# Moving a join: Fourier matmuls ahead of the last z tiles, and a third bank for the decay exponents

## The chip, the cores and the metric

The kernel runs on one core of a Trainium2 chip. The metric is the device time of one execution in microseconds. A core has a matrix engine (TensorE, PE in the profile), three engines for elementwise work (VectorE or DVE, ScalarE or ACT, GpSimd or POOL) and a synchronising engine (SyncE or SP), from whose queue this kernel issues every DMA. Matmul results go to PSUM, which has eight banks of 512 float32 columns for each of the 128 partitions; all other tiles lie in SBUF.

## The reference

One layer of a diffusion backbone over 2048 latent tokens with a prefix of 256 context tokens. The input is normalised and projected to 5168 columns (u, zf, zs, x/B/C, dt). The Fourier group takes the real part of a two-dimensional DFT of u, a linear map, and a gate silu(zf). The other group runs a 3x3 depthwise convolution and a bidirectional chunked state-space scan with 24 heads in four groups, gated with silu(zs) and normalised in groups. Both are joined and projected once more, with a residual and a last norm.

```python
decay within a chunk:  y_diag = (C B^T * exp(segsum(a))) x
decay from the state:  y_off  = C h * exp(a_cum)
gated  = (y_f + y_b + d_skip * x) * silu(zs)
ssd    = gated * rsqrt(mean(gated^2) + eps) * norm_w      # mean over 384 channels of a group
four   = (real(fft2(u)) @ w_fourier + b_fourier) * silu(zf)
out    = rmsnorm(x + gate * ([four, ssd] @ w_out)) * final_norm_w
```

## The kernel before, in words

Matrix products that need float32 accuracy are made of three matmuls on values that are split into a high and a low part (`hi*hi + lo*hi + hi*lo`). So a weight tile is loaded raw (`raw`, one buffer of 512 KB), ACT copies its high part (`wh`) and POOL subtracts to the low part (`wl`); the normalised input lies in `hh` and `hl` in four blocks of 512 tokens each.

The stages are: context; projections of dt and of the scan's inputs; convolution; the backward scan, with z tiles (the projection to zs, 128 channels by 512 tokens each, 24 matmuls) of the blocks 0 to 2 interleaved; the Fourier part, with the 12 z tiles of block 3 interleaved; and the last stage. Before that last stage the split columns of the output projection, 32 loads of 512 KB, are read back from DRAM (`wo_d`) into the places of `hh` and `hl` that have become free (`wplace`, four groups of eight loads, `w_group(g)`).

The Fourier part has a first step (`f_table`, `f_step2`; the L923 transforms) and 16 calls `f_mm(dt, h, i)` of 12 matmuls (L941 to L943); after each second call `f_gate` (L951, L960) multiplies into `zf`, which was loaded by `zf_load` from `zfT_d`, and after the last of a `dt` the result, 1 MB, is stored to `fm_d`. `interleave(main, side, lead, speed, finish)` writes the operations of two lists in turn by a table of costs; what of the side list is not placed comes back as `left`.

The last stage goes over 16 chunks times 4 groups, 64 units u. Each has six steps. `s1`: loads; the decay exponents as two matmuls for each half (`parg`, L1079), joined by a predicated copy on DVE (L1081), exponential on ACT (L1083), product with C B^T on DVE (w, L1084). `s2`: loads; the part from the state (`pyo`, L1115 to L1117), scaled (L1119) and added to the backward part on POOL (L1120). `s3`: the state update (`pst`, L1136 to L1138). `s4`: y of the unit, 12 matmuls and three transposes that add the part of s2 (`py`, L1151 and L1154), then the gate on DVE (`gt`, L1157), squares on ACT, a reduction on DVE. `s5`: the norm. A matmul with ones sums over the partitions (`pn`, L1167), ACT takes a root by three activations (L1170 to L1172), DVE mends it by two instructions (L1173, L1174) that write into pn, and multiplies the gated tile by it (L1176); the product is split into `mh` and `ml`. `s6`: the unit's share of the output projection, 24 matmuls (`po`, L1210 to L1212), from mh, ml and the Fourier operand `fm`. The loop writes s1 and s2 of u+1, s3 and s4 of u, s5 of u-1 and s6 of u-2 in each turn.

The written order isn't the executed one: a scheduler orders the instructions of each engine by its own estimate of durations, under the dependencies of the tiles. A tile with `bufs=1` may be written again only when its last reader is done. `issue_after(x)` holds loads back behind x. Each engine keeps its order on the chip.

In the last stage the eight PSUM banks are: parg 2, po 2, pyo 2 (with pst), py 1, pn 1.

Of the kernel before, what the change touches and what calls it, by code (L numbers as in the profile page):

```python
# [18 lines left out]
P = 128  # L19
D = 1024  # L20
# [29 lines left out]
def mixer_layer(ctx: ExitStack, tc: tile.TileContext, A: dict, out: bass.AP, taps=None):  # L50
# [797 lines left out]

    wos = {}
    worder = [k for g in range(G) for k in (4 + 3 * g, 5 + 3 * g, 6 + 3 * g, g)]  # L850
    wplace = [((hl, 1536), (hh, 1536)), ((hl, 0), (hl, 1024)), ((hl, 512), (hh, 1024)), ((hh, 0), (hh, 512))]

    def w_load(n):
        r, k = 2 * (n % 4), worder[n]
# [4 lines left out]
    def w_group(g):  # L859
        for n in range(4 * g, 4 * g + 4):  # L860
            w_load(n)
# [148 lines left out]
    for b in range(4):  # L1010
# [5 lines left out]
    side.append((0.0, f_switch))  # L1016
    fmm = [(dt, h) for dt in dts[:2] for h in range(2)] + [(dt, h) for h in range(2) for dt in dts[2:]]
    for n, (dt, h) in enumerate(fmm):
        if n in (4, 5):
            side.append((0.0, zf_load(dt)))  # L1020
        if n == 6:
            side.append((0.0, lambda: w_group(1)))
# [23 lines left out]
    ps = pool("ps2", space=PSUM)  # L1046
    fo["new"] = lambda: ps.tile([P, 512], F32, name="pft", tag="out", bufs=2)
    pre2 = preload(LNEXP)
    units = {}

    def s1(u):
# [16 lines left out]
        cb = wa1.tile([P, P], F32, name="cb", tag="cb")  # L1068
        load(cb, cb_d[c, :, g])
        chl = wa1.tile([P, 2, P], F32R, name="chl", tag="chl")  # L1070
        load(chl[:].bitcast(F32), chl_d[c, :, g].bitcast(F32))
        d["chl"] = chl
        w = wa1.tile([P, HG, P], F32, name="w", tag="w")
        for h2 in range(2):
            cols = slice(384 * h2, 384 * h2 + 384)
            pa = []
            for dr in range(2):
                po = ps.tile([P, 3, P], F32, name="parg", tag="arg", bufs=2)
                mm(po, l[:, dr], r[:, cols], start=True, stop=True)  # L1079
                pa.append(po)  # L1080
            nc.vector.copy_predicated(out=pa[0], mask=msk[:].unsqueeze(1).broadcast_to([P, 3, P]), data=pa[1])  # L1081
# [7 lines left out]
    pfb.close()  # L1089
    p1w.close()  # L1090
    wk = pool("wk", 2)
    fnw = const_tile("fnw", wk)
    wa = pool("wa", 2)

    def s2(u):
        c, g = divmod(u, G)
        d = units[u]
        gs = slice(g * GW, (g + 1) * GW)
        yb = wa1.tile([P, HG, 64], F32, name="yb4", tag="yb")
        load(yb[:].rearrange("p h w -> p (h w)"), yb_d[c, :, gs])  # L1100
        zs = wa1.tile([P, 3, P], F32, name="zs4", tag="zs")
        load(zs, zsT_d[c, :, 3 * g:3 * g + 3, :])
        d["zs"] = zs
        xg = wa1.tile([P, HG, 64], F32, name="xg", tag="xg", bufs=3)
        load(xg[:].rearrange("p h w -> p (h w)"), xtok_d[c, :, gs])
        d["x"] = xg
        bt = wa1.tile([P, 2, P], F32R, name="bt4", tag="bt", bufs=2)
        d["ld"] = load(bt[:].bitcast(F32), bhl_d[c, :, g].bitcast(F32))
        d["b"] = bt
# [5 lines left out]
        mm(po, d["chl"][:, 0], sh, start=True, stop=False)  # L1115
        mm(po, d["chl"][:, 0], sl, start=False, stop=False)
        mm(po, d["chl"][:, 1], sh, start=False, stop=True)  # L1117
        ec = d["sml"][:, 2, g * HG:(g + 1) * HG].unsqueeze(2).broadcast_to([P, HG, 64])
        nc.vector.tensor_tensor(out=ts, in0=po, in1=ec, op=ALU.mult)  # L1119
        nc.gpsimd.tensor_tensor(out=ts, in0=ts, in1=yb, op=ALU.add)  # L1120
        d["ts"] = ts

    def s3(u):
# [21 lines left out]
    def s4(u):  # L1145
        c, g = divmod(u, G)
        d = units[u]
        py = ps.tile([P, 3, P], F32, name="py", tag="yT", bufs=1)
        for h in range(HG):
            o = 64 * (h % 2)  # L1150
            mm(py[o:o + 64, h // 2, :], d["x"][:, h], d["w"][:, h], start=(h < 2), stop=False, skip_group_check=True)  # L1151
        tsf = d["ts"][:].rearrange("p h w -> p (h w)")
        for j in range(3):
            mm(py[:, j, :], tsf[:, j * P:(j + 1) * P], ident, is_transpose=True, start=False, stop=(j == 2),  # L1154
               skip_group_check=True)
        gt = wk.tile([P, 3, P], F32, name="gt", tag="gt")
        nc.vector.scalar_tensor_tensor(out=gt, in0=py, scalar=-1.0, in1=d["zs"], op0=ALU.mult, op1=ALU.mult)  # L1157
        sq = wk.tile([P, 3, P], F32, name="sq4", tag="sq", bufs=1)
        nc.scalar.activation(sq, gt, AF.Square)
        s0 = wk.tile([P, P], F32, name="s0", tag="s0", bufs=1)  # L1160
        nc.vector.tensor_reduce(out=s0, in_=sq[:].rearrange("p j l -> p l j"), axis=AX.X, op=ALU.add)
        d["gt"], d["sq"] = gt, s0

    def s5(u):
        d = units[u]
        pn = ps.tile([P, P], F32, name="pn", tag="misc", bufs=1)
        mm(pn, ones, d["sq"], start=True, stop=True)  # L1167
        rs = wk.tile([P, P], F32, name="rs4", tag="rs", bufs=1)
        tt = wk.tile([P, P], F32, name="tt", tag="tt", bufs=1)
        nc.scalar.activation(rs, pn, AF.Ln, bias=eps_t[:, 0:1], scale=1.0 / GW)  # L1170
        nc.scalar.activation(rs, rs, AF.Exp, scale=-0.5)
        nc.scalar.activation(tt, rs, AF.Square, scale=math.sqrt(0.5 / GW))  # L1172
        nc.vector.scalar_tensor_tensor(out=pn, in0=pn, scalar=EPS * GW, in1=tt, op0=ALU.add, op1=ALU.mult)  # L1173
        nc.vector.scalar_tensor_tensor(out=pn, in0=pn, scalar=1.5, in1=rs, op0=ALU.subtract, op1=ALU.mult)  # L1174
        mx = d["gt"]
        nc.vector.tensor_tensor(out=mx, in0=mx, in1=pn[:].unsqueeze(1).broadcast_to([P, 3, P]), op=ALU.mult)  # L1176
# [14 lines left out]
    def s6(u):  # L1191
# [14 lines left out]
        for i, q in [(i, q) for i in range(2) for q in range(4)] if (u > NU-2) else [(i, q) for q in range(4) for i in range(2)]:  # L1206
                k, a, b = ops[q]
                wh, wl = wos[k]
                po = ost["po"][i]
# [38 lines left out]
    for u in range(NU + 2):  # L1248
        if u + 1 < NU:
            if u > 0:  # L1250
                s1(u + 1)
            s2(u + 1)
        if u < 2:
            with tc.issue_after(fo["st"]), tc.issue_after(units[u + 1]["ld"]):
                w_group(u + 2)
        if u < NU:
            s3(u)
            s4(u)
        if 1 <= u <= NU:
            s5(u - 1)  # L1260
        if u >= 2:
            s6(u - 2)
# [110 lines left out]
```

## Time and profile before

| | |
|---|---|
| runs | 1903.54, 1904.05, 1899.87 us; median 1903.54 |
| profiled execution | 1907.05 us, its span 1905.3 us, mean granted PE clock 0.978 |
| PE busy | 1810.8 us, 95% of the span |
| DVE, ACT, POOL busy | 1259.1, 874.9, 904.0 us |
| DMA | 301.8 MB, 158 GB/s in the mean |
| last stage | from 1260 us to the end |

In the rows of the profile a line such as `L1151` is one of the kernel before. `out<-in` names the tiles, `x12` counts instructions that were merged into a row, `[15.64 <-DVE yy L951]` is the engine's idle time ahead of the row and what ended it. A stretch's row gives its length, then for PE, PE's weight loads, DVE, ACT and POOL the busy time with the count of instructions, then the clock that PE was granted (1.00 is full speed), the share of the DMA engines and GB/s.

### The profile page before, as it was taken

To read this page: it belongs to the slowest core of one execution; us is meant where nothing else is said; L and a number is where in the kernel's file an instruction comes from. 1 tells how busy PE (TensorE), PEld (TensorE's weight loads), DVE (VectorE), ACT (ScalarE), POOL (GpSimd) and SP (SyncE) were. 2 spreads that over 40 slices of the span, in tenths; PEclk is the share of its full clock that TensorE was granted. 3 is DMA by queue.
4 is the path that set the end of the run, shared out by engine and by line. 5 is a ranking of instruction groups with operands and counts; after the bars stand their busy time and mean duration, and the time that the engine had idled before them with its cause. 6 is when DMAs were issued, how large, how long until landed. Compare 5 with 4: busy or idle time off the path is not lost.

```text
span 1905.3 us, 28132 instructions
## 1 busy us (share of the span) xinstructions
PE 1810.8 (95%) x9142; PEld 1495.8 (79%) x9142; DVE 1259.1 (66%) x1809; ACT 874.9 (46%) x1968; POOL 904.0 (47%) x791
## 2 busy tenths in 40 slices
PE   7989999999999999999999999957999999999997
PEld 3779988888888888788888877845778777777875
DVE  4744578888898887556666622334677777767865
ACT  4532244445445445347666643312444444434443
POOL 2320034223124133178788723235777777668742
PEclk9999999999999999999999999977999999999999
DMA  8332345445446245467777764786444444444441
GB/s 306 127 95 78 96 135 169 144 130 160 128 125 194 90 138 159 143 196 216 209 218 212 221 232 136 245 277 208 123 146 149 130 132 135 148 122 137 145 136 48
DMA packets 291332, 301.80 MB, mean 158 GB/s; under 512 B 34098, under 2 KB 242066, under 8 KB 290675
## 3 DMA queue, kind: packets, MB, share of 16 engines
q1 hardware_dynamic: 291186, 300.01, 50.6%
q8 instruction: 73, 1.20, 0.3%
q14 instruction: 73, 0.59, 0.1%
HBM read 196.82 MB, written 103.10 MB: 157 GB/s over the span
## 4 chain that ended last, share of the span: by engine, by line
PE 72%; DMA 9%; POOL 4%; DVE 3%; issue 2%; ACT 2%; SPq 1%; POOLq 0%; ACTq 0%; DVEq 0%
PE pj L178 11%; PE pj L177 11%; PE pj L176 11%; PE po L1212 6%; PE po L1210 6%; PE po L1211 6%; PE py L1151 2%; PE parg L1079 2%; POOL sl L72 2%; PE pj L508 1%; PE pj L509 1%; PE pj L510 1%; PE py L1154 1%; DMA ev<-in_wout 1%; PE ptr L569 1%
## 5 line engine op out<-in xcount | busy, mean ns | idle before, releaser
L178 PE MATMUL pj<-hh,wl 128*128 128x512 f32 x1152 | 453.9, 394 | 0.8 <-POOL wl L72 0.8
L176 PE MATMUL pj<-hh,wh 128*128 128x512 f32 x1152 | 450.7, 395 | 3.9 <-ACT img L68 2.1
L177 PE MATMUL pj<-hl,wh 128*128 128x512 f32 x1152 | 453.3, 393 | 0.0
L636 DVE SCALAR_TENSOR_TENSOR pacc<-img,c_convw,pacc 128x1024 f32<-128x1024 f32 x320 | 410.4, 1288 | 60.2 <-ACT pacc L633 50.7
L72 POOL TENSOR_TENSOR wl<-raw,wh 128x1024 fp32r<-128x1024 f32 x48 | 115.6, 2409 | 348.7 <-ACT wh L68 296.2
L178 PEld LDWEIGHTS pj<-hh,wl 128*128 128x128 f32 x1152 | 217.2, 189 | 48.3 <-issue 1.6
L176 PEld LDWEIGHTS pj<-hh,wh 128*128 128x128 f32 x1152 | 217.4, 189 | 46.7 <-ACT img L68 3.2
L177 PEld LDWEIGHTS pj<-hl,wh 128*128 128x128 f32 x1152 | 217.4, 189 | 40.3 <-issue 1.0
L807 ACT ACTIVATE xd<-xt,smb 128x64 f32<-128x64 f32 x384 | 100.9, 336 | 80.1 <-POOL yb L811 78.7
L1210 PE MATMUL po<-hl,mh 128*128 128x512 f32 x288 | 118.7, 412 | 1.0 <-DVE og L1224 0.6
L1211 PE MATMUL po<-hh,mh 128*128 128x512 f32 x288 | 115.0, 399 | 0.0
L1081 DVE COPY_PREDICATED parg<-msk,parg 128x384 f32<-128x384 uint8 x128 | 71.2, 556 | 65.9 <-PE parg L1079 65.4
L1212 PE MATMUL po<-hl,ml 128*128 128x512 f32 x288 | 110.6, 403 | 2.5 <-POOL ml L72 2.4
L1083 ACT ACTIVATE w<-parg 128x384 f32<-128x384 f32 x128 | 62.2, 486 | 108.3 <-DVE parg L1081 108.0
L72 DVE TENSOR_TENSOR xl<-xw,xh 128x384 fp32r<-128x384 f32 x76 | 63.7, 842 | 59.4 <-ACT xh L68 58.0
L1120 POOL TENSOR_TENSOR ts<-ts,yb 128x384 f32<-128x384 f32 x64 | 73.3, 1145 | 57.9 <-issue 30.4
L1079 PE MATMUL parg<-rt,lt 128*128 128x384 f32 x256 | 87.7, 371 | 11.8 <-DMA lt<-q_d 7.5
L72 POOL TENSOR_TENSOR ml<-gt,mh 128x384 fp32r<-128x384 f32 x64 | 68.2, 1065 | 58.9 <-ACT mh L68 55.5
L68 ACT ACTIVATE xh<-xw 128x384 fp32r<-128x384 f32 x136 | 70.0, 516 | 50.2 <-PE pst L1138 17.0
L1084 DVE TENSOR_TENSOR w<-w,cb 128x768 f32<-128x768 f32 x64 | 81.0, 1265 | 12.0 <-ACT w L1083 10.8
L72 POOL TENSOR_TENSOR sl<-ev,sh 128x512 fp32r<-128x512 f32 x32 | 42.4, 1324 | 89.6 <-DMA wo_d<-sl 36.0
L72 DVE TENSOR_TENSOR sl<-hbk,sh 128x384 fp32r<-128x384 f32 x64 | 60.0, 939 | 37.4 <-ACT sh L68 37.3
(388 smaller groups left out, 4131.9 us busy)
## 6 DMA issues: line engine op xcount, KB each, us to landing
raw<-in_win SPq DMA_DIRECT2D x48, 512.0 KB
xt<-xtok_d SPq DMA_DIRECT2D x80, 192.0 KB
xtok_d<-tk SPq DMA_DIRECT2D x48, 256.0 KB
zsT_d<-ev SPq DMA_DIRECT2D x48, 256.0 KB
yb_d<-yb SPq DMA_DIRECT2D x64, 192.0 KB
yb<-yb_d SPq DMA_DIRECT2D x64, 192.0 KB
zs<-zsT_d SPq DMA_DIRECT2D x64, 192.0 KB
xg<-xtok_d SPq DMA_DIRECT2D x64, 192.0 KB
```

The source lines that it names most:

```text
L72: (lo_engine or nc.vector).tensor_tensor(out=lo, in0=src, in1=hi.bitcast(F32), op=ALU.subtract)
L176: mm(po, wh[:, k], a, start=(k == 0), stop=False)
L177: mm(po, wh[:, k], b, start=False, stop=False)
L178: done["mm"] = mm(po, wl[:, k], a, start=False, stop=(k == KT - 1)).ins
L636: nc.vector.scalar_tensor_tensor(out=acc, in0=im[:, r0 + dy:r0 + dy + 16, dx:dx + GRID_W], scalar=tap(t), in1=acc, op0=ALU.mult, op1=ALU.add)
L807: nc.scalar.activation(xd[:, h], d["x"][:, h], AF.Copy, scale=smb[:, 3, c, g * HG + h:g * HG + h + 1])
L1079: mm(po, l[:, dr], r[:, cols], start=True, stop=True)
L1084: nc.vector.tensor_tensor(out=w, in0=w, in1=cb[:].unsqueeze(1).broadcast_to([P, HG, P]), op=ALU.mult)
L1120: nc.gpsimd.tensor_tensor(out=ts, in0=ts, in1=yb, op=ALU.add)
L1210: mm(po, a, wh[:, i], start=(g == 0 and q == 0), stop=False)
L1211: mm(po, a, wl[:, i], start=False, stop=False)
L1212: mm(po, b, wh[:, i], start=False, stop=(g == 3 and q == 3))
```

## The change

Four parts. (1) The Fourier preparation is interleaved with the z tiles 0 to 4 of the 12, the 16 `f_mm` calls with the tiles 5 to 7, and the tiles 8 to 11 come last; under them go the loads of the output projection's groups 0 and 1. `wplace` is reordered, so that block 3's columns, which those last tiles still read, belong to group 3. Loads of the first units stand ahead of the last tiles, for which the loads are split out of `s1` and `s2` (`s1_load`, `s2_load`). Groups 2 and 3 are held back behind the units' loads, and no longer behind the Fourier store. `fnw` is loaded in the third turn. (2) parg gets a third bank (`arg0` two, `arg1` one). (3) pn has no bank of its own: `py` becomes four times 128 columns, and pn of unit u-1 is written in the fourth of py of unit u. (4) s6 takes the Fourier operand first, and the last unit's order follows.

```diff
-    wplace = [((hl, 1536), (hh, 1536)), ((hl, 0), (hl, 1024)), ((hl, 512), (hh, 1024)), ((hh, 0), (hh, 512))]
+    wplace = [((hl, 0), (hl, 1024)), ((hl, 512), (hh, 1024)), ((hh, 0), (hh, 512)), ((hl, 1536), (hh, 1536))]
...
-    left = interleave(zs_ops([(i, (3,)) for i in range(19, 7, -1)]), side, 10, .75)
+    ztiles = list(zs_ops([(i, (3,)) for i in range(19, 7, -1)]))
+    ztiles = [ztiles[n:n + KT + 1] for n in range(0, len(ztiles), KT + 1)]
+    zrun = lambda a, b: [op for t in ztiles[a:b] for op in t]
+    interleave(zrun(0, 5), side, 8, 1, True)
+    f_switch()
+    side = []
...
         side += [(2.6, f_mm(dt, h, i)) for i in range(2)]
+        if n in (1, 3):
+            side.append((0.0, zf_load(dts[2 + n // 2])))
+    interleave(zrun(5, 8), side, 0, 1, True)
...
-    w_group(0)
-    for _, fn in left:
-        fn()
-    p1.close()
...
+    s1_load(0)
+    s2_load(0)
+    s1_load(1)
+    interleave(zrun(8, 12), [(1.0, lambda n=n: w_load(n)) for n in range(8)], 0, 1, True)
+    p1.close()
+    ps = pool("ps2", space=PSUM)
+    pre2 = preload(LNEXP)
...
-                po = ps.tile([P, 3, P], F32, name="parg", tag="arg", bufs=2)
+                po = ps.tile([P, 3, P], F32, name="parg", tag=f"arg{dr}", bufs=2 - dr)
...
-    fnw = const_tile("fnw", wk)
+    fnw = wk.tile([P, D], F32, name="c_fnw", bufs=1)
...
-        py = ps.tile([P, 3, P], F32, name="py", tag="yT", bufs=1)
+        py = d["py"] = ps.tile([P, 4, P], F32, name="py", tag="yT", bufs=1)
...
-        pn = ps.tile([P, P], F32, name="pn", tag="misc", bufs=1)
+        pn = (units[u + 1]["py"] if u + 1 < NU else ps.tile([P, 4, P], F32, name="py", tag="yT", bufs=1))[:, 3]
...
-        ops = [(4 + 3 * g + j, d["mh"][:, j], d["ml"][:, j]) for j in range(3)] + [(g, fm[:, 0, g % 2], fm[:, 1, g % 2])]
+        ops = [(g, fm[:, 0, g % 2], fm[:, 1, g % 2])] + [(4 + 3 * g + j, d["mh"][:, j], d["ml"][:, j]) for j in range(3)]
...
         if u + 1 < NU:
             if u > 0:
+                s1_load(u + 1)
                 s1(u + 1)
+            s2_load(u + 1)
             s2(u + 1)
-        if u < 2:
-            with tc.issue_after(fo["st"]), tc.issue_after(units[u + 1]["ld"]):
-                w_group(u + 2)
+            if u < 2:
+                with tc.issue_after(units[u + 1]["ld"]):
+                    w_group(u + 2)
+            if u == 2:
+                load(fnw, A["fnw"])
```

How the instructions stand is seen at two places. The first is the SP queue at the join. Of the kernel before, where all raw weights have been issued by then:

```order
L63 DMA fm_d<-zf 128x16x128
L63 DMA hl<-wo_d 128x2x512 x8
L63 DMA zf<-zfT_d 128x2048
L63 DMA fm_d<-zf 128x16x128 x2
L63 DMA hl<-wo_d 128x2x512
```

Of the change, up to the raw weights of z tile 10; the raw weights of tile 9 stand four rows above the first of these, with two hl loads and an hh load between:

```order
L63 DMA hh<-wo_d 128x2x512
L63 DMA fm_d<-zf 128x16x128
L63 DMA hl<-wo_d 128x2x512
L63 DMA hh<-wo_d 128x2x512 x4
L63 DMA hl<-wo_d 128x2x512
L63 DMA hh<-wo_d 128x2x512 x2
L63 DMA hl<-wo_d 128x2x512
L63 DMA hh<-wo_d 128x2x512 x3
L63 DMA zsT_d<-ev 128x4x128
L63 DMA hh<-wo_d 128x2x512
L63 DMA fm_d<-zf 128x16x128
L63 DMA raw<-in_win 128x1024
```

The loads of the groups 0 to 2, 24 of 512 KB, now stand among and ahead of the last raw weights: 17 of them, two fm_d stores and a zsT store lie between the raw weights of tile 9 and those of tile 10. Between those of tile 10 and 11 follow two zsT stores, fnw, one fr and two xr loads.

The second is PE in the last stage, around one pn and the py after it. Before, pn (the row with `c_ones`) waits for the reduction on DVE, and 18 matmuls of po, parg and pyo follow up to the next py:

```order
L1211 MATMUL po_13714<-hh,mh 128x512
L1167 MATMUL pn<-s_13697,c_ones 128x128 [waits DVE_49]
L1212 MATMUL po_13714<-hl,ml 128x512
L1210 MATMUL po_13713<-hl,mh 128x512
L1211 MATMUL po_13713<-hh,mh 128x512
L1212 MATMUL po_13713<-hl,ml 128x512
```

Of the change:

```order
L1222 MATMUL po_13696<-hl,fm 128x512
L1099 MATMUL parg<-rt_11320,lt_11322 128x384 [waits DVE_49]
L1176 MATMUL py<-s_13543,c_ones 128x128 [waits DVE_49]
L1124 MATMUL pyo<-sh_13982,chl 128x384 [waits DMAHW4_49,DVE_49]
L1125 MATMUL pyo<-sl_13983,chl 128x384
L1126 MATMUL pyo<-sh_13982,chl 128x384
L1099 MATMUL parg<-rt_11319,lt_11321 128x384 [waits DMAHW6_49,DMAHW1_49,DMAHW7_49,DMAHW0_49,DVE_49]
L1160 MATMUL py<-w,xg 64x128 [waits DVE_49,PE_49]
L1160 MATMUL py<-w,xg 64x128 x5
L1163 MATMUL py<-c_ident,ts 128x128 x3
```

The sum with ones now writes the tile py; three pyo and one parg stand between it and the next unit's py, where 18 matmuls stood. In the other units it is between one and some twenty matmuls.

More of the change, by code (lines that the diff above doesn't have):

```diff
@@ L1015, in mixer_layer @@
             side += [(0.0, zf_load(dt)) for dt in dts[:2]]
[L1016 to L1022, printed above, removed]
+    ztiles = list(zs_ops([(i, (3,)) for i in range(19, 7, -1)]))
[4 more added lines that the diff above has]
+    side = []
+    for n, (dt, h) in enumerate([(dt, h) for dt in dts[:2] for h in range(2)] +
+                                [(dt, h) for h in range(2) for dt in dts[2:]]):
         side += [(2.6, f_mm(dt, h, i)) for i in range(2)]
-    left = interleave(zs_ops([(i, (3,)) for i in range(19, 7, -1)]), side, 10, .75)
+        if n in (1, 3):
+            side.append((0.0, zf_load(dts[2 + n // 2])))
+    interleave(zrun(5, 8), side, 0, 1, True)
     wa1 = P2["wa1"]
@@ L1040, in mixer_layer, with s1_load @@
         nc.vector.tensor_copy(out=t, in_=st2[:, :2])
-    w_group(0)
-    for _, fn in left:
-        fn()
-    p1.close()
-    ps = pool("ps2", space=PSUM)
-    fo["new"] = lambda: ps.tile([P, 512], F32, name="pft", tag="out", bufs=2)
-    pre2 = preload(LNEXP)
     units = {}
-    def s1(u):
+    def s1_load(u):
         c, g = divmod(u, G)
@@ L1067, in s1, with s2_load @@
                 load(l[32 * dr + 6 * s:32 * dr + 6 * s + 6, dr].bitcast(F32), q_d[s, hsl, cs].bitcast(F32))
[L1068 to L1072, printed above, removed]
+        d["cb"] = wa1.tile([P, P], F32, name="cb", tag="cb")
+        load(d["cb"], cb_d[c, :, g])
+        d["chl"] = wa1.tile([P, 2, P], F32R, name="chl", tag="chl")
+        load(d["chl"][:].bitcast(F32), chl_d[c, :, g].bitcast(F32))
+    def s2_load(u):
+        c, g = divmod(u, G)
+        d = units[u]
+        gs = slice(g * GW, (g + 1) * GW)
+        d["yb"] = wa1.tile([P, HG, 64], F32, name="yb4", tag="yb")
+        load(d["yb"][:].rearrange("p h w -> p (h w)"), yb_d[c, :, gs])
+        d["zs"] = wa1.tile([P, 3, P], F32, name="zs4", tag="zs")
+        load(d["zs"], zsT_d[c, :, 3 * g:3 * g + 3, :])
+        d["x"] = wa1.tile([P, HG, 64], F32, name="xg", tag="xg", bufs=3)
+        load(d["x"][:].rearrange("p h w -> p (h w)"), xtok_d[c, :, gs])
+        d["b"] = wa1.tile([P, 2, P], F32R, name="bt4", tag="bt", bufs=2)
+        d["ld"] = load(d["b"][:].bitcast(F32), bhl_d[c, :, g].bitcast(F32))
+    s1_load(0)
[5 more added lines that the diff above has]
+    pre2 = preload(LNEXP)
+    def s1(u):
+        d = units[u]
+        cb, r, l = d["cb"], rt[u % 2], lt[u % 2]
         w = wa1.tile([P, HG, P], F32, name="w", tag="w")
@@ L1119, in s2 @@
         nc.vector.tensor_tensor(out=ts, in0=po, in1=ec, op=ALU.mult)
-        nc.gpsimd.tensor_tensor(out=ts, in0=ts, in1=yb, op=ALU.add)
+        nc.gpsimd.tensor_tensor(out=ts, in0=ts, in1=d["yb"], op=ALU.add)
         d["ts"] = ts
@@ L1156, in s4 @@
         gt = wk.tile([P, 3, P], F32, name="gt", tag="gt")
-        nc.vector.scalar_tensor_tensor(out=gt, in0=py, scalar=-1.0, in1=d["zs"], op0=ALU.mult, op1=ALU.mult)
+        nc.vector.scalar_tensor_tensor(out=gt, in0=py[:, :3], scalar=-1.0, in1=d["zs"], op0=ALU.mult, op1=ALU.mult)
         sq = wk.tile([P, 3, P], F32, name="sq4", tag="sq", bufs=1)
@@ L1175, in s5 @@
         mx = d["gt"]
-        nc.vector.tensor_tensor(out=mx, in0=mx, in1=pn[:].unsqueeze(1).broadcast_to([P, 3, P]), op=ALU.mult)
+        nc.vector.tensor_tensor(out=mx, in0=mx, in1=pn.unsqueeze(1).broadcast_to([P, 3, P]), op=ALU.mult)
         mh = wk.tile([P, 3, P], F32R, name="mh", tag="mh", bufs=2)
@@ L1204, in s6 @@
             fm_half(*divmod(u // 2 + 1, 2))
-        ops = [(4 + 3 * g + j, d["mh"][:, j], d["ml"][:, j]) for j in range(3)] + [(g, fm[:, 0, g % 2], fm[:, 1, g % 2])]
-        for i, q in [(i, q) for i in range(2) for q in range(4)] if (u > NU-2) else [(i, q) for q in range(4) for i in range(2)]:
+        ops = [(g, fm[:, 0, g % 2], fm[:, 1, g % 2])] + [(4 + 3 * g + j, d["mh"][:, j], d["ml"][:, j]) for j in range(3)]
+        for i, q in ([(0, 0), (1, 0)] + [(i, q) for i in range(2) for q in range(1, 4)] if u > NU - 2
+                     else [(i, q) for q in range(4) for i in range(2)]):
                 k, a, b = ops[q]
```

11 lines of the change are left out of this document (removed).

## The prediction

> **What bounds the kernel now.** I read the page first, then the busy time in stretches, then the waits and the timeline of the two places that the change touches. The page says that TensorE (PE) is the bound, and that its granted clock dips once in the last third of the span, in the 27th and 28th of the 40 slices.
>
> ```profile
> PE 1810.8 (95%) x9142; PEld 1495.8 (79%) x9142; DVE 1259.1 (66%) x1809; ACT 874.9 (46%) x1968; POOL 904.0 (47%) x791
> PEclk9999999999999999999999999977999999999999
> ```
>
> Those slices are the join between the Fourier part and the last stage. Stretches of 20 us over it, and the whole last stage (columns: length, busy time of PE, weight loads, DVE, ACT, POOL, then PEclk, DMA share, GB/s):
>
> ```profile
> 1240.00:1260.00 20.00, 4.93 (x23) 3.83 (x21) 4.15 (x7) 0.60 (x1) 4.79 (x6) 0.76 0.68 248
> 1260.00:1280.00 20.00, 15.59 (x64) 11.94 (x65) 11.38 (x18) 5.76 (x13) 10.07 (x10) 0.65 1.01 330
> 1280.00:1300.00 20.00, 7.53 (x33) 5.28 (x32) 6.54 (x13) 5.40 (x13) 6.37 (x6) 0.61 0.78 264
> 1300.00:1320.00 20.00, 17.66 (x73) 14.32 (x73) 7.03 (x13) 4.81 (x10) 10.88 (x11) 0.71 0.63 192
> 1320.00:1340.00 20.00, 20.00 (x113) 16.23 (x112) 13.42 (x26) 10.51 (x26) 16.81 (x17) 1.00 0.48 141
> 1320.00:1900.00 580.00, 559.62 (x3085) 447.74 (x3083) 416.45 (x767) 258.90 (x661) 391.94 (x371) 0.99 0.43 130
> ```
>
> Work at full clock, stretch by stretch, is busy time by clock: 4.93 x .76 + 15.59 x .65 + 7.53 x .61 + 17.66 x .71 = 3.7 + 10.1 + 4.6 + 12.5 = 31 us in 80. So the join costs about 49 us, some 34 of it idle and the rest half speed. The waits say why: PE sat 15.64 us for the Fourier output, which waited for zf, and zf stood in the one SP queue behind eight loads of the output projection's weights; 7.5 us more went to lt, behind the next eight.
>
> ```profile
> 1260.57 0.66 PE L1115 MATMUL pyo<-sh,chl 128*128 128x384 f32 x1 [15.64 <-DVE yy L951]
> ```
> ```profile
> 1233.92 8.24 SPq L63 DMA_DIRECT2D hl<-wo_d  x8
> ```
> ```profile
> 1242.64 12.67 DMA zf<-zfT_d
> ```
> ```profile
> PE parg L1079 <- DMA lt<-q_d: 7.5, 2, 5.5
> ```
>
> The last stage runs 64 units, and there PE is nearly gapless. The sixth unit's py and the last unit's begin at
>
> ```profile
> 1335.46 0.77 PE L1151 MATMUL py<-w,xg 128*64 128x128 f32 x10
> ...
> 1877.49 0.88 PE L1151 MATMUL py<-w,xg 128*64 128x128 f32 x12 [0.52 <-issue]
> ```
>
> so a unit takes (1877.49 - 1335.46) / 58 = 9.35 us. What its matmuls need back to back follows from starts in an undisturbed place:
>
> ```profile
> 1855.24 0.34 PE L1117 MATMUL pyo<-sh,chl 128*128 128x384 f32 x1
> 1855.42 0.52 PE L1079 MATMUL parg<-rt,lt 128*128 128x384 f32 x2
> 1855.87 0.88 PE L1151 MATMUL py<-w,xg 128*64 128x128 f32 x12
> 1856.67 0.55 PE L1154 MATMUL py<-c_ident,ts 128*128 128x128 f32 x3
> 1856.98 0.59 PE L1079 MATMUL parg<-rt,lt 128*128 128x384 f32 x2
> ...
> 1863.27 0.40 PE L1212 MATMUL po<-hh,ml 128*128 128x512 f32 x1
> 1863.51 0.39 PE L1210 MATMUL po<-hh,mh 128*128 128x512 f32 x1
> ```
>
> A 384-column matmul takes .18 us, the twelve of py .80, its three transposes .31, a 512-column one .235. Per unit: 24 po x .235 + 10 of 384 columns x .18 + .80 + .31 and about .15 for the two of pn = 8.7 us. The stage thus loses .65 us a unit.
>
> **The change part by part.** *1. The join.* PE work is the same, in another order: four z tiles now come after the last Fourier matmul (99 z matmuls at the .23 us pitch, 22.5 us), where before 15.64 us of idleness stood. Two things eat this cover. First, the new order of the SP queue puts 17 weight loads of the output projection (groups 0, 1 and, against its place in the code, 2), two fm_d stores and a zsT store between the raw weights of z tile 10 and those of tile 9. The rates while such transfers run alone, and the split of a raw tile into wh and wl:
>
> ```profile
> 1244.00:1248.00 4.00, 0.93 (x5) 0.53 (x3) 0.00 (x0) 0.00 (x0) 0.00 (x0) 1.00 1.05 392
> 1260.00:1264.00 4.00, 3.43 (x11) 3.27 (x11) 3.64 (x6) 1.31 (x3) 1.93 (x2) 0.52 0.95 263
> ```
> ```profile
> L72 POOL TENSOR_TENSOR wl<-raw,wh 128x1024 fp32r<-128x1024 f32 x48 | 115.6, 2409 | 348.7 <-ACT wh L68 296.2 <-PE ptr L569 52.5
> L68 ACT ACTIVATE wh<-raw 128x1024 fp32r<-128x1024 f32 x48 | 50.6, 1054 | 48.4 <-DMA raw<-in_win 24.8 <-PE pj L177 23.6
> ```
>
> A load of 512 KB at 392 GB/s is 1.35 us, a store of 1 MB at 263 GB/s 4.0. Seventeen loads, two stores, .7 for zsT and the raw tile itself are 23 + 8 + 2 = 33 us, of which I let 3.5 run before the last Fourier matmul ends. Raw tile 10 is then in at about +29, wh and the first of wl at +32, while PE has work from the last Fourier matmul to +11.6 (51 matmuls). That is some 20 us of new idleness, some 2 for tile 11 (its raw buffer is the same one, and fnw, fr and two xr, 1.1 MB, lie ahead of it), and about 2 at a cold clock. Second, the ramp of the first unit stands after the z tiles as it stood after the Fourier part: last z evacuation, exponential, w, py, gt, sq, reduce, pn, mh follow one another. Before, from the first pyo above to the first po with mh went 14 us:
>
> ```profile
> 1274.81 0.80 PE L1210 MATMUL po<-hl,mh 128*128 128x512 f32 x1 [0.39 <-ACT mh L68]
> ```
>
> I estimate 16 with the evacuation, against which PE has about a unit's work, 8.5: 8 us idle and 2 to 5 at half clock. Together 35 to 38 against the 49 of before: **join -10**, bounds -30 (raw tiles in time) and 0 (a raw stall of 30 us instead of 20).
>
> *2. pn in py's bank, all 64 units.* Before, pn had a bank of its own and followed nothing but the reduction; now pn of unit u-1 lies in the tile of py(u). So pn(u-1) waits until gt(u) has read py(u), and py(u+1), which takes the same one buffer, waits until the product with pn(u-1) is formed. What lies between, in a unit of before:
>
> ```profile
> 1322.19 0.38 PE L1167 MATMUL pn<-s,c_ones 128*128 128x128 f32 x2
> ...
> 1322.62 0.37 ACT L1170 ACTIVATE rs<-pn,eps_t 128x128 f32<-128x128 f32 x1 [0.43 <-PE pn L1167]
> ...
> 1323.02 0.31 ACT L1171 ACTIVATE rs<-rs 128x128 f32<-128x128 f32 x1
> ...
> 1323.36 0.31 ACT L1172 ACTIVATE tt<-rs 128x128 f32<-128x128 f32 x1
> ...
> 1323.70 0.30 DVE L1173 SCALAR_TENSOR_TENSOR pn<-pn,tt 128x128 f32<-128x128 f32 x1
> ...
> 1324.04 0.30 DVE L1174 SCALAR_TENSOR_TENSOR pn<-pn,rs 128x128 f32<-128x128 f32 x1
> ...
> 1324.61 0.56 DVE L1081 COPY_PREDICATED parg<-msk,parg 128x384 f32<-128x384 uint8 x1 [0.28 <-PE parg L1079]
> ...
> 1325.08 0.55 DVE L1176 TENSOR_TENSOR gt<-gt,pn 128x384 f32<-128x384 f32 x1
> ```
>
> From pn's start to the product's end: 3.44 us with another DVE instruction in between; without it the product would start .34 after L1174 as the others do, 1324.38 + .55, that is 2.74. With some .1 to PE's release: 2.85 to 3.5. PE keeps its program order, and in the new order only these stand between a pn and the next py: for instance one parg and three pyo and one parg (.9 us), the same with pst (2.3 with po), 1.58 us in the mean over 62 units, counted row by row with the durations above. Before, 2.3 us up to more than a unit lay there, and py did not depend on pn. PE thus stalls 2.85 - W, taken unit by unit and never below zero, 1.3 us in the mean; with 3.5 it is 1.9 to 2.0. A unit becomes at least 8.7 + 1.3 = 10.0, or 8.7 + 2.0 = 10.7: **+.65 to +1.35 x 58 = +38 to +78, I take +58**, the middle, since by the row of the whole stage ACT is busy for 259 of 580 us and DVE for 416, so that other units' work stands in the chain's way often, not always. Nothing hides it: what is behind py in PE's queue is the transposes, po and parg, and for those everything else waits. The waits of before are not added: py's stall covers them.
>
> *3. The clock.* The new gaps of 1.3 to 2 us are of the size of three of before:
>
> ```profile
> 1349.78 0.69 PE L1136 MATMUL pst<-xh,bt 128*128 128x384 f32 x1 [1.48 <-DVE ts L1119]
> ...
> 1669.33 0.74 PE L1212 MATMUL po<-hl,ml 128*128 128x512 f32 x2 [1.67 <-POOL ml L72]
> ...
> 1859.33 0.44 PE L1079 MATMUL parg<-rt,lt 128*128 128x384 f32 x1 [1.75 <-DVE parg L1081]
> ```
> ```profile
> 1350.00:1354.00 4.00, 4.00 (x13) 3.63 (x14) 3.60 (x7) 2.86 (x8) 4.00 (x5) 0.50 0.66 205
> 1670.00:1674.00 4.00, 4.00 (x12) 3.10 (x11) 0.88 (x2) 1.36 (x3) 3.75 (x5) 0.57 0.51 141
> 1860.00:1864.00 4.00, 4.00 (x21) 3.28 (x20) 2.98 (x5) 1.90 (x5) 0.54 (x1) 1.00 0.07 19
> ```
>
> After the first two PE ran at half speed for four us or so and lost about 2 us each; after the third, the longest, it did not. I take one drop in ten units in the likeliest case, since the gap that was longest cost nothing, 6 x 2 = **+12**, and keep 0 and one in each unit for the range.
>
> The Trainium skill, TensorE: Matmul & The Clock Gate, section HAM oscillation — how this bites in real kernels, puts the limit at idle gaps of PE of about 3.4 us. The half speed behind the gaps of 1.48 and 1.67 us contradicts it. By that rule the term would be 0, the forecast 12 us lower, at 1952, and rival B could not be.
>
> *4. The rest.* The third bank for parg lets one more exponent matmul run ahead; its worth is at most a part of the .65 us a unit lost before, and nothing while py's wait is longer. Taking the Fourier operand first in the output projection gives six matmuls, 1.4 us, before mh is needed, which ahead of a py stall only moves idleness. The last unit's new order is under 1 us either way, fnw's load is hidden.
>
> **The sum.** The profiled execution took 1907.05 us around its span of 1905.3: 1907 - 10 + 58 + 12 = 1967. It lies 3.5 us above the median of 1903.54, so I give **1964 us**.
>
> **Rivals.** *A. The stall is hidden and the join pays (other side: faster).* It takes one thing: that W and the chain match so that a unit stays at 9.35, for which the stall must be .65 or less, thus a chain of 2.2 us at the mean W of 1.58, or W 2.2. Then the .65 lost before and the stall are the same idleness, and what is left is the join, -10 to -30: 1873 to 1893, say 1885. For it: the third bank and the early Fourier operand take other waits out of PE's way. Against it: the shortest chain in the rows is 2.74. *B. Half clock becomes the rule.* Each stall is followed by four us at half speed, 2 us lost, and the stall shrinks by up to .8 as the work in W takes longer: 58 x 1.2 = +70 on top of -10 and +58: 1903.5 + 118 = 2022. For it: two of three gaps; against: the third. *C. The raw tiles come in time,* since the queue moves loads faster than 392 GB/s or the last z tiles find their weights earlier: join -30, steady +58 and +12: 1944. *D. The change cancels out,* join -30 with steady +30 or so: within 4 us of 1903.5.
>
> **How the numbers follow.** The forecast (1930 to 1995, C within it at 1944) has .55, of which C .12; B .22 (1995 to 2045); A .17; D .06. The likeliest is 1964. The range must reach into A and B to leave out no more than 2 in 10: 1888 to 2035; the likeliest case's own is 1930 to 1995. A difference of .2%, about 4 us, is what a measurement of this kernel can tell: faster .18, same .05, slower .77.
>
> **What would show it.** In the changed kernel's waits, PE py <- DVE gt (the product) should lead the last stage with 60 to 120 us over some 60 times, and its py should start every 10.0 to 10.7 us. At the join, PE (or ACT's wh) should wait about 20 us for raw<-in_win, then some 8 for the first unit's chain. PEclk in the last stage should be .95 to .99; below .9 it is B. I am wrong if the unit's period is 9.4 or less, or if no wait for raw stands at the join.

## The result, and the profile after

The changed kernel takes 1987.58 us in the median (four runs, 1987.37 to 1990.99) against 1901.88 us (1899.87 to 1904.05) before: a ratio of 1.0448, with a 95% interval of 1.0433 to 1.0463. It is slower, by 86 us; forecast were 60 slower, and the range of 1888 to 2035 us holds it.

The page of the changed kernel, PE's line and the granted clock:

```profile
PE 1827.9 (92%) x9142; PEld 1500.9 (76%) x9142; DVE 1239.8 (62%) x1809; ACT 872.4 (44%) x1968; POOL 896.5 (45%) x791
PEclk9999999999999999999999999789999999999998
```

PE has the same 9142 instructions, busy 17 us more (some at a lower clock), in a span that is 80.4 us longer. The same 500 us of the last stage in stretches, first after, then before (PE's busy time is the second number; the third from the end is the granted clock):

```profile
1340.00:1840.00 500.00, 442.23 (x2363) 349.79 (x2361) 307.45 (x593) 198.63 (x511) 309.17 (x300) 0.97 0.40 120
```
```profile
1340.00:1840.00 500.00, 485.87 (x2694) 389.99 (x2693) 370.58 (x679) 229.07 (x584) 360.76 (x342) 0.99 0.46 137
```

PE now sits idle for 58 of 500 us where it was 14. One DVE instruction a unit reads py (gt); its start marks a unit. The sixth and the last of them, after and before:

```profile
1335.88 0.56 DVE L1166 SCALAR_TENSOR_TENSOR gt<-py,zs 128x384 f32<-128x384 f32 x1 [2.62 <-PE py L1163]
...
1957.57 0.56 DVE L1166 SCALAR_TENSOR_TENSOR gt<-py,zs 128x384 f32<-128x384 f32 x1 [1.72 <-POOL ml L72]
```
```profile
1336.92 0.56 DVE L1157 SCALAR_TENSOR_TENSOR gt<-py,zs 128x384 f32<-128x384 f32 x1 [0.18 <-PE py L1154]
...
1880.80 0.54 DVE L1157 SCALAR_TENSOR_TENSOR gt<-py,zs 128x384 f32<-128x384 f32 x1
```

So the span's 80.4 us divide without a rest: the sixth unit's mark comes 1.0 us earlier, the 58 units after it take 621.7 instead of 543.9 us (10.72 against 9.38 each, +77.8), and from the last mark to the end it is 28.1 instead of 24.5 us (+3.6). The unit of every run below is taken from these marks in the same way. The waits of PE in the changed kernel's last stage, from 1330 us on (us in total, times, longest), and at the join:

```profile
PE py L1160 <- DVE gt L1185: 52.4, 49, 2.2
PE pyo L1124 <- DVE hf L1151: 8.8, 19, 0.7
PE po L1220 <- DVE og L1234: 5.2, 15, 1.9
PE py L1160 <- issue: 4.6, 2, 2.4
```
```profile
PE pj L176 <- ACT wh L68: 22.0, 1, 22.0
```

Both places that the prediction named are there. L1185 is the product with pn (a line number in a row is one of that run's own kernel). The prediction expected this wait at 60 to 120 us over some 60 times; it is 52.4 us in 49. One such stall in the timeline (the rows from pn to the next py, with others left out):

```profile
1612.36 0.39 PE L1176 MATMUL py<-s,c_ones 128*128 128x128 f32 x2
...
1612.78 0.37 ACT L1179 ACTIVATE rs<-py,eps_t 128x128 f32<-128x128 f32 x1
...
1613.18 0.31 ACT L1180 ACTIVATE rs<-rs 128x128 f32<-128x128 f32 x1
...
1613.81 0.29 ACT L1181 ACTIVATE tt<-rs 128x128 f32<-128x128 f32 x1
...
1614.14 0.30 DVE L1182 SCALAR_TENSOR_TENSOR py<-py,tt 128x128 f32<-128x128 f32 x1 [0.19 <-ACT tt L1181]
1614.47 0.30 DVE L1183 SCALAR_TENSOR_TENSOR py<-py,rs 128x128 f32<-128x128 f32 x1
1614.80 0.55 DVE L1185 TENSOR_TENSOR gt<-gt,py 128x384 f32<-128x384 f32 x1
...
1615.50 0.88 PE L1160 MATMUL py<-w,xg 128*64 128x128 f32 x12 [1.88 <-DVE gt L1185]
```

From pn's start to the next py go 3.14 us, in which PE had three pyo and one parg, 1.26 us with pn itself; the other 1.88 it was idle. That is the shortest kind: by the rows of the whole stage, py waited for the product in 50 of the 62 units that have a pn ahead of them and a py behind, and from pn's start to py it took 3.13 to 3.94 us there, 3.48 in the mean. At the join the raw weights are the late ones:

```profile
1242.38 11.07 DMA raw<-in_win
```

Their issue begins at 1242.38, behind the weight loads and the stores, and they land 11.07 us later; PE had run out of work at 1232.6.

### The profile page after: what moved, and what is told of

It reads as the page before. It is cut to its first block, busy times and chain, and to the rows that moved or that the text cites. A ratio compares the mean times of both kernels' runs of the same rounds, so it can differ in the third digit from the quotient of the medians.

```text
span 1985.7 us, 28122 instructions
## 1 busy us (share of the span) xinstructions
PE 1827.9 (92%) x9142; PEld 1500.9 (76%) x9142; DVE 1239.8 (62%) x1809; ACT 872.4 (44%) x1968; POOL 896.5 (45%) x791
## 4 chain that ended last, share of the span: by engine, by line
PE 68%; DMA 6%; DVE 6%; issue 4%; ACT 4%; POOL 4%; SPq 1%; ACTq 0%; POOLq 0%; DVEq 0%
PE pj L178 10%; PE pj L177 10%; PE pj L176 10%; PE po L1220 6%; PE po L1221 6%; PE po L1222 6%; PE py L1160 3%; DMA raw<-in_win 2%; PE py L1163 2%; POOL sl L72 1%; DVE gt L1185 1%; PE pj L508 1%; PE pj L509 1%; PE pj L510 1%; PE ptr L569 1%
## 5 line engine op out<-in xcount | busy, mean ns | idle before, releaser
L1220 PE MATMUL po<-hl,mh 128*128 128x512 f32 x288 | 123.9, 430 | 0.0
L1160 PE MATMUL py<-w,xg 128*64 128x128 f32 x768 | 59.8, 292 | 59.1 <-DVE gt L1185 53.9
L1170 DVE TENSOR_REDUCE s<-sq 128x128 f32<-128x384 f32 x64 | 38.0, 594 | 118.2 <-PE py L1176 118.2
L1160 PEld LDWEIGHTS py<-w,xg 128*64 128x64 f32 x768 | 45.0, 143 | 77.9 <-issue 61.0
L72 POOL TENSOR_TENSOR sl<-hf,sh 128x384 fp32r<-128x384 f32 x64 | 65.5, 1024 | 76.6 <-ACT sh L68 76.2
L72 POOL TENSOR_TENSOR xl<-xw,xh 128x384 fp32r<-128x384 f32 x60 | 62.0, 1033 | 83.2 <-ACT xh L68 83.1
L1099 PE MATMUL parg<-rt,lt 128*128 128x384 f32 x256 | 93.0, 377 | 6.1 <-DVE parg L1101 4.5
L1128 DVE TENSOR_TENSOR ts<-pyo,sml 128x384 f32<-128x384 f32 x64 | 35.6, 556 | 80.6 <-PE py L1163 80.6
```

What stands on the lines that cost most here:

```text
L72: (lo_engine or nc.vector).tensor_tensor(out=lo, in0=src, in1=hi.bitcast(F32), op=ALU.subtract)
L1220: mm(po, a, wh[:, i], start=(g == 0 and q == 0), stop=False)
```

## The experiments

**1. pn in its own bank again.** Everything of the change but the PSUM banks.

```diff
-                po = ps.tile([P, 3, P], F32, name="parg", tag=f"arg{dr}", bufs=2 - dr)
+                po = ps.tile([P, 3, P], F32, name="parg", tag="arg", bufs=2)
...
-        py = d["py"] = ps.tile([P, 4, P], F32, name="py", tag="yT", bufs=1)
+        py = ps.tile([P, 3, P], F32, name="py", tag="yT", bufs=1)
...
-        pn = (units[u + 1]["py"] if u + 1 < NU else ps.tile([P, 4, P], F32, name="py", tag="yT", bufs=1))[:, 3]
+        pn = ps.tile([P, P], F32, name="pn", tag="misc", bufs=1)
...
```

> The changed kernel with the PSUM banks of before: two banks for parg, and pn in a bank of its own. The order of the Fourier part, of the z tiles, of the loads and of the output projection's operands stays as changed. Theory (pn in py's bank makes every unit longer): the unit goes from 10.7 back to about 9.4 us, no wait of py for the product with pn is left, the 22 us wait for raw weights at the join stays, so 1898 to 1908 us. Rival (the new order of operands and loads costs the time, not the bank): it stays above 1960. Rival 2 (the third parg bank was worth something by itself): between 1910 and 1930.

Measured: 1892.58 us, .994 of before (.9925 to .9955), unit 9.21 us. No wait of py for the product is left in the last stage; the wait at the join is as long as in the changed kernel:

```profile
PE po L1220 <- ACT mh L68: 3.2, 2, 2.8
PE parg L1099 <- DVE parg L1101: 2.6, 3, 1.1
```
```profile
PE pj L176 <- ACT wh L68: 22.5, 1, 22.5
```

The banks cost the changed kernel 95 us (1987.58 less 1892.58), more than its whole loss; the rest of the change is a gain of .6%, 5 us beyond the expected range.

**2. The banks alone,** in the kernel before, the same lines the other way.

> The kernel before with the PSUM banks of the change alone: three banks for parg, pn in py's bank. In its new order 1.58 us of PE work stand between a pn and the next unit's py in the mean, as in the changed kernel. Theory: the unit goes from 9.4 to 10.7 us, 1975 to 1990 us in all, with py's wait for the product leading the waits. Rival (it is the other parts that cost): 1895 to 1910.

Measured: 2026.14 us, 1.0642 of before (1.0625 to 1.0658), unit 11.29 us. The cause is confirmed, the size was missed by 36 us. A second wait is large here, that of pyo for the state's sum (`hf`), 30.5 us against 8.8:

```profile
PE py L1151 <- DVE gt L1176: 62.7, 56, 1.9
PE pyo L1115 <- DVE hf L1142: 30.5, 40, 1.1
```

The clock in 1340 to 1840 us was .95. The banks alone cost 123 us, within the change 95. The longer wait of pyo, 22 us more than in the changed kernel, is of the size of that difference; why pyo waits longer here was not tried.

**3. Two py banks in turn,** pn still in py's, two banks for parg.

```diff
-                po = ps.tile([P, 3, P], F32, name="parg", tag=f"arg{dr}", bufs=2 - dr)
+                po = ps.tile([P, 3, P], F32, name="parg", tag="arg", bufs=2)
...
-        py = d["py"] = ps.tile([P, 4, P], F32, name="py", tag="yT", bufs=1)
+        py = d["py"] = ps.tile([P, 4, P], F32, name="py", tag="yT", bufs=2)
...
```

> The changed kernel with pn still in py's bank, but two such banks in turn and two for parg. py of unit u+2 now waits for the product with pn of u-1; since the order again puts pn late, 2.07 us of PE work in the mean stand between them where 1.58 stood, and pn still waits for the gate's read. Theory (the stall is the chain's length less that work): taken row by row with a chain of 2.85 to 3.5 us the stall is 1.1 to 1.7 us a unit where the changed kernel's was 1.3 to 1.95, so the unit takes 10.1 to 10.5 us and the run 1945 to 1975 us. Rival (any second buffer cures it): about 1902. Rival (pn's own wait for the gate in the shared bank is what costs): no change, 1985 to 1990.

Measured: 1997.15 us, 1.049 (1.0472 to 1.0508), unit 10.78 us: none of the three. py's wait did fall, from 52 to 22 us, but others took its place:

```profile
PE parg L1099 <- DVE parg L1101: 23.7, 39, 1.8
PE py L1160 <- DVE gt L1185: 21.7, 34, 1.4
PE po L1220 <- DVE og L1234: 11.5, 14, 1.9
PE py L1160 <- PE parg L1099: 7.2, 9, 0.8
```

The rule "chain less the PE work between" prices the wait at py, not the stall as a whole. A parg that stands ahead of py now needs a bank that DVE's predicated copy frees. Whether that is the two parg banks or the late place of pn was left to runs 10 and 11.

**4. Own bank, and raw weights ahead of weight loads.** Run 1, with the loads queued behind the last raw weights that were written ahead of them (`done["raw"]` is the last such load so far).

```diff
...
+    def w_held(n):
+        with tc.issue_after(done["raw"]):
+            w_load(n)
...
-    interleave(zrun(8, 12), [(1.0, lambda n=n: w_load(n)) for n in range(8)], 0, 1, True)
+    interleave(zrun(8, 12), [(1.0, lambda n=n: w_held(n)) for n in range(8)], 0, 1, True)
...
-                with tc.issue_after(units[u + 1]["ld"]):
+                with tc.issue_after(units[u + 1]["ld"]), tc.issue_after(done["raw"]):
```

> As the first run (PSUM banks of before in the changed kernel), and in addition the output projection's weight loads are held in the queue behind the raw weights that stand ahead of them in the written order; the third group is held behind the last raw weights. Between the raw weights of z tile 9 and 10 stand six such loads instead of 17. Theory (the 22 us wait for raw weights is queueing): the wait falls to 0 to 4 us, and the run is 15 to 20 us shorter than the first run, 1880 to 1890 us. Rival (the same bytes are only waited for later, by the first units' loads or the output projection's weights): within 5 us of the first run.

Measured: 1878.31 us, .9869 (.9853 to .9885); 14.3 us less than run 1, just short of the expected 15 to 20, and 1.7 us below the range of 1880 to 1890, since run 1 itself came out lower than expected. PE's waits at the join:

```profile
PE parg L1103 <- DMA lt<-q_d: 4.7, 1, 4.7
PE pj L176 <- ACT wh L68: 4.3, 2, 2.9
PE pj L178 <- POOL wl L72: 3.1, 2, 1.7
```

Of the 22.5 us 18 went, and a few came back as waits for wl and lt. So the stall at the join was queueing, and 14.3 of these 18 us were gained in the run.

**5. Same banks as changed, another order on PE.** The output projection of unit u-2, but for the Fourier operand, is queued behind pn of unit u-1.

```diff
+        d["pni"] = mm(pn, ones, d["sq"], start=True, stop=True).ins
...
+            with ExitStack() as hold:
+                if q and u + 1 < NU:
+                    hold.enter_context(tc.issue_after(units[u + 1]["pni"]))
                 mm(po, a, wh[:, i], start=(g == 0 and q == 0), stop=False)
...
```

> The changed kernel with every PSUM bank as changed (three for parg, pn in py's bank); only the order on PE is held: of the output projection of unit u-2, all but the Fourier operand's matmuls is queued behind pn of unit u-1. Between a pn and the next unit's py then stand 6.3 us of PE work in the mean instead of 1.58, and between py's end and pn 1.2 us. Theory (the stall is the part of the chain pn to product that PE's own queue doesn't cover; the shared bank as such is harmless): py's wait for the product falls from 52 us to under 8, the unit from 10.72 to 9.0 to 9.5 us, the run to 1885 to 1915 us. Rival (pn's wait for the gate's read in the same bank, or the exclusion of two engines from one bank, takes the place): a new wait of pn for the gate of .5 to 1 us a unit, 1930 to 1970 us.

Measured: 1903.87 us, 1.0007 (.9996 to 1.0019), unit 9.43 us, clock 1.00. No wait of py for the product is left in the stage, though pn lies in py's bank as in the changed kernel: it was PE's order under that tie that made the loss. The unit is back to the 9.38 us of before, not to the 9.21 of run 1. The rival's wait exists, at about half its price:

```profile
PE py L1176 <- DVE gt L1166: 16.2, 30, 1.0
PE parg L1099 <- DVE parg L1101: 3.9, 13, 0.5
```

That is pn (now a part of py) waiting for the gate's read of the same tile, 16 us in all, .28 us a unit where .5 to 1 was named.

**6. The same with the raw weights ahead.**

> The held order of the run before this one, with the weight loads held behind the raw weights as in the fourth run. Against the fourth run (1878 us, own bank for pn, two banks for parg, unit 9.17 us) it shows what the third parg bank is worth once pn does no harm. Theory: the third bank takes away parg's waits for the predicated copy, about 1 us in all there, so nothing: 1873 to 1890 us. Rival (the third bank lets PE run ahead and is worth .2 us a unit or more): under 1868 us.

Measured: 1893.13 us, .9953 (.9938 to .9968), unit 9.42 us: 15 us behind run 4 and above the expected range. With the third parg bank, pn in py's bank and the held order it is slower than with none of them. pn's wait for the gate, 16.4 us here, is of the size of that difference; that it is the cause was not tried.

**7. A third parg bank, and pn in the banks of pyo.** Run 4 with

```diff
-                po = ps.tile([P, 3, P], F32, name="parg", tag="arg", bufs=2)
+                po = ps.tile([P, 3, P], F32, name="parg", tag=f"arg{dr}", bufs=2 - dr)
...
-        pn = ps.tile([P, P], F32, name="pn", tag="misc", bufs=1)
+        pn = ps.tile([P, P], F32, name="pn", tag="yo", bufs=2)
```

> The fourth run with a third bank for parg, and pn as a tile of its own in the two banks that pyo and the state update take in turn, so that pn is tied to these instead of to py. Theory: the third bank is worth nothing measurable (as above), and pn in that turn ties a unit's state matmuls to the chain's end, with the scheduler's order putting some 3 us between: 1876 to 1900 us. Rival: the third bank pays, below 1868 us.

Measured: 1865.0 us, .98 (.9776 to .9824), the fastest of all, 13.3 us below run 4. The time is the one that the rival named; that the third bank alone makes it is not shown, since pn's place changed with it. No wait of PE is left from 1340 us to the end, and 500 of 500 us are busy at full clock, at 9.01 us a unit:

```profile
PE 1800.2 (97%) x9142; PEld 1489.9 (80%) x9142; DVE 1254.2 (67%) x1809; ACT 873.3 (47%) x1968; POOL 886.3 (48%) x791
```

That pyo and the state update free their two banks early enough for pn, where py doesn't free its one, is how I read it. pn in pyo's banks with only two for parg was not run.

**8. mh first again,** run 4 with the operand order of before (and that of the last unit).

```diff
-        ops = [(g, fm[:, 0, g % 2], fm[:, 1, g % 2])] + [(4 + 3 * g + j, d["mh"][:, j], d["ml"][:, j]) for j in range(3)]
+        ops = [(4 + 3 * g + j, d["mh"][:, j], d["ml"][:, j]) for j in range(3)] + [(g, fm[:, 0, g % 2], fm[:, 1, g % 2])]
...
```

> The fourth run with the output projection's operands in the order of before (mh, ml first, the Fourier operand last; the last unit's order too). The unit of the first and fourth runs is 9.2 us where it was 9.38 before. Theory (the Fourier operand first, six matmuls or 1.4 us of slack before mh, is what gained that): the unit goes back to about 9.38 and the run is 8 to 14 us longer than the fourth, 1886 to 1893 us. Rival (the loads' new order gained it): within 4 us of the fourth.

Measured: 1893.0 us, .9946 (.9927 to .9965), unit 9.40 us. The Fourier operand first is worth 14.7 us, at the upper end of what was expected. The waits that come back are the ones that led the last stage of the kernel before (there 5.6 and 2.4 us):

```profile
PE pst L1149 <- DVE ts L1132: 4.5, 7, 1.0
PE po L1225 <- POOL ml L72: 3.2, 4, 1.7
```

In the 58 units between the marks PE is idle for 20 us where it was 10 in run 4. Added up over stretches of 2 us, busy time less busy time by clock is 5 us where it was nothing.

**9. The least mend.** The changed kernel with only pn's place altered to that of run 7.

> The changed kernel with one thing altered: pn is a tile of its own in the two banks that pyo and the state update take in turn, not the fourth part of py's. Three banks for parg, the loads and the raw weights' wait at the join stay as changed. Theory: the whole of the loss hangs on the tie of pn to py, and the third bank is worth what the run with it gained over the fourth (13 us): the unit takes 9.0 us, the wait of 22 us for raw weights stays, 1876 to 1886 us. Rival (the gain of that run needed the weight loads' order too): above 1890.

Measured: 1874.35 us, .9857 (.9841 to .9874), 1.7 us below the expected range; unit 9.07 us, with a wait of 20.9 us for raw weights at the join. In the stage

```profile
1340.00:1840.00 500.00, 500.00 (x2814) 404.74 (x2814) 378.11 (x701) 235.63 (x603) 346.25 (x343) 1.00 0.47 140
```

One tile's place thus turns 86 us of loss into 28 of gain. Against run 1 (two parg banks, pn in its own) it is 18 us. The spans of the two profiled executions differ by 22.5 us; of these 12.4 come before the sixth unit, for which no cause was looked for, 7.8 in the units after it and 2.3 at the end.

**10. Two parg banks, pn in py's one bank.**

```diff
-                po = ps.tile([P, 3, P], F32, name="parg", tag=f"arg{dr}", bufs=2 - dr)
+                po = ps.tile([P, 3, P], F32, name="parg", tag="arg", bufs=2)
```

> The changed kernel with two parg banks in place of three, pn in py's one bank as changed. 1.86 us of PE work stand between a pn and the next py in the mean (1.58 as changed). If the run with two py banks was slow because two parg banks put the wait for DVE on parg instead of py, then parg's wait for the predicated copy grows here from 4.5 to 15 us or more, and the run is 1985 to 2005 us. If the stall is only the chain less the PE work between, it is .3 us a unit shorter than as changed: 1965 to 1978 us.

Measured: 1985.97 us, 1.0445 (1.0411 to 1.0478), the same as with three. The first reading was right by its waits:

```profile
PE py L1160 <- DVE gt L1185: 27.2, 41, 2.1
PE parg L1099 <- DVE parg L1101: 18.4, 29, 1.1
```

The third bank gains nothing under the tie: it only moves the stall from parg to py. Where the scheduler orders PE freely, the runs leave the tie of pn to py as the cause of the loss: with it 1986 and 1988 us (two parg banks, run 10, and three, the changed kernel), without it 1893 and 1874 (two, run 1, and three, run 9).

**11. Run 3 with the held order of run 5.**

> The run with two py banks in turn and two for parg, with the output projection of unit u-2 (but the Fourier operand's matmuls) queued behind pn of unit u-1. Some 15 us of PE work then stand between a pn and the py that waits for its product. If PE's place for pn sets both waits, py's and parg's, both fall under 5 us and the run is 1885 to 1915 us. If the two parg banks cost by themselves in this order, parg's wait for the copy stays at 15 us or more: 1915 to 1950 us.

Measured: 1885.39 us, .9916 (.9901 to .9931), unit 9.08 us. py's wait for the product is gone, and parg's is

```profile
PE parg L1099 <- DVE parg L1101: 5.1, 12, 1.1
```

against 23.7 us in run 3, a hair above the 5 us that was named. So it was pn's late place on PE that set both waits of run 3, not the number of parg banks.

## Why the prediction was right

It named the cause, the place and the sign, and the runs bear all three out. By its own steps, compared by the spans of the profiled executions (forecast +60, measured +80.4; by the medians it is 86, as the profiled execution of before lay 5 us above its median):

- **pn in py's bank, +58 (38 to 78).** Right, and the largest term. PE's busy time between the two marks, first after, then before:

```profile
1335.88:1957.57 621.69, 546.34 (x2927) 431.30 (x2927) 378.14 (x733) 243.24 (x625) 363.01 (x351) 0.97 0.39 117
```
```profile
1336.92:1880.80 543.88, 526.77 (x2919) 421.25 (x2918) 399.43 (x733) 246.22 (x628) 374.20 (x355) 0.99 0.44 133
```

PE was idle for 75.4 us where it had been 17.1, +58.2. That this is the very number is partly luck, for the parts of the working were off and cancelled. PE's need of a unit was counted as 8.7 us from the starts; runs 7 and 9, with PE never idle, show 9.0 to 9.1, so before the change only .37 us a unit was lost, not .65. The chain was put at 2.85 to 3.5 us and took 3.13 to 3.94. The work under it was counted as 1.58 us in the mean; in the 50 units that stalled, 2.4 us went by before PE fell idle for py (3.48 less a mean wait of 1.08). So the stall at py, put at 1.3 to 1.95 us a unit, was .9. The idle time of 1.3 us a unit is reached only with the other waits, those for hf, og and parg above all, of which the working had none ("py's stall covers them").

- **The clock, +12.** Right in kind and near in size. Of the 25 gaps of .9 us and more after 1330 us, ten were followed by four us at a clock of .57 to .66; (1 - .61) x 4 x 10 = 16 us. Added up over stretches of 2 us between the marks, busy time less busy time by clock is 15 us, where it was 5 before: +11. So there was about one drop in six units at 1.6 us, where one in ten at 2 was forecast. Together the two terms were 70 and measured 69 of the 77.8 us in those 58 units. The other 9 us are busy time at full clock, and stay unexplained.
- **The join, -10.** The pieces were right: PE out of work 11.7 us after the last Fourier matmul (forecast 11.6), the raw weights in after 32.5 (29), a stall of 22.0 us (20). In 20 us stretches from 1220 to 1340 us, worked out as the prediction did it for before, the changed kernel loses 47 us; 5.7 of the last 40 us are the stage's ordinary loss (idle and clock of the row over 500 us), which leaves 42 where 35 to 38 were forecast, -7 instead of -10. The net at the sixth unit is -1, and what was off is the count of units: the stall was charged to the 58 from the sixth on, but the first five have it too.
- **The rest, nothing.** The tail costs 3.6 us. The last unit's new order, put at "under 1 us either way", is not what costs it: in run 1, which has that order, the tail is 23.6 us, .9 shorter than before. What the working left out is the last pn: with no next py to lie in, it takes py's one bank as a new tile and waits for the product before it, 2.55 us by its row.

```profile
1965.67 0.46 PE L1176 MATMUL py<-s,c_ones 128*128 128x128 f32 x2 [2.55 <-DVE gt L1185]
```

Two remarks hold at most under the tie. The Fourier operand first "only moves idleness": with the tie that was not tried, without it the order is worth 14.7 us (run 8). The third bank is worth "nothing while py's wait is longer": run 10 bears that out (1985.97 against 1987.58 us). Without the tie it was run only together with pn in pyo's banks; the two gained .14 to .16 us a unit (run 9 against 1, 7 against 4) and took all of PE's waits in the stage, which nothing in the traces of before had shown to be possible.

Rival A (the stall hidden) fell with the 52.4 us and with run 1, B (half clock as a rule) with the ten in 25, C (raw weights in time) with the 22.0 us. What stays open is why the banks alone cost 123 us and within the change 95, beyond the longer wait of pyo.

## What to carry to other kernels

In this kernel two tiles in one PSUM bank were one tile for whoever had to wait. Before a narrow result is put into the free columns of another's bank, follow the chain from its write to its last read, and see what on the in-order engine stands behind the bank's next write: the chain took 3.1 to 3.9 us here, and PE stood idle for what it had no other work to fill. The two banks of pyo for pn (run 9), or 6.3 us of other work queued behind pn (run 5), took that wait away; the second left pn waiting .28 us a unit for the gate. A wait that is eased at one place can come back at another, as run 3 shows, so count all of the engine's waits and not only the first. And a DMA that is moved earlier in a queue pushes everything behind it: 17 weight loads ahead of one load of raw weights left PE idle for 22 us. Look at what the last loads of the stage before are queued behind.

## What the hardware showed that was not expected

Half speed after gaps of equal length was not the same each time. Two gaps of 1.88 us in the changed kernel, and the four us after each:

```profile
1615.50:1619.50 4.00, 4.00 (x22) 3.25 (x23) 1.89 (x3) 1.81 (x4) 1.38 (x2) 0.65 0.76 234
1659.05:1663.05 4.00, 4.00 (x28) 3.33 (x29) 2.61 (x4) 1.81 (x4) 2.40 (x3) 1.00 0.79 243
```

Of 14 gaps of 1.88 or 1.89 us eight were followed by a clock under .7 and six by 1.00; of six of 1.19 us one was, and of the four longest, 2.21 to 2.55 us, one. Nearly all stand ahead of py, at the same place of the loop. In run 2, with the banks alone, all thirteen gaps of 1.88 or 1.89 us were followed by a clock under .7, and four of the fourteen of 1.18 or 1.19. So in these two kernels a gap of 1.9 us made the drop likely, not sure, and a longer one no surer. The Trainium skill, TensorE: Matmul & The Clock Gate, section HAM oscillation — how this bites in real kernels, puts the limit at about 3.4 us of idleness; these traces show drops at about half of that, and they decide here. The same page of the Trainium skill, section Part 1: The HAM clock gate (the "warmup" mystery) says that the window over which activity is watched runs freely. That would fit equal gaps with unequal ends; no run here tests it.
